# Reading the first half of an output projection out of PSUM: one VectorE addition, or a ScalarE copy and a POOL addition

## The chip, the cores and the metric

The kernel runs on one NeuronCore of a Trainium2 chip. The metric is the time of one execution on the device in microseconds (us), the median over several runs. The core's engines are TensorE (PE: matmuls and transposes, which write to PSUM), VectorE (DVE), ScalarE (ACT), GpSimd (POOL) and the DMA queues, most of them issued by SyncE (SP). Each engine works through its own queue of instructions in order and waits for the others by semaphores. PSUM holds the results of PE in eight banks; SBUF holds everything else.

## The reference, cut to what matters

Two layers of a decoder trunk on x of 512 tokens by 1024 features in float32. Each layer has one input projection, three groups of heads beside each other, one output projection that is added to x, and a SwiGLU feed-forward block that is added to x.

```python
for l in range(DEPTH):                                   # DEPTH = 2
    h = rmsnorm(x, attn_norm[l])
    (q, kc, vc, ksl, ...) = split_columns(h @ w_in[l])
    o_nsa = nsa_mixer(...)                               # 512 features: attention
    o_gla = gla_mixer(...)                               # 256 features: linear attention
    o_sg = spatial_gating(...)                           # 256 features
    x = x + jnp.concatenate([o_nsa, o_gla, o_sg], axis=-1) @ w_out[l]
    h = rmsnorm(x, ffn_norm[l])
    x = x + (jax.nn.silu(h @ w_gate[l]) * (h @ w_up[l])) @ w_down[l]
return rmsnorm(x, final_norm)
```

The rows of `w_out` that belong to o_gla and o_sg (the second 512 of 1024) need nothing of o_nsa. That half of the product can be computed while attention still runs.

## The kernel before, in words

x is kept transposed in SBUF for the whole kernel, in the tile `xT`: 8 blocks of 128 features by 512 tokens, float32. Matrix products are made with split operands: a weight block of 128 x 1024 is loaded into a tile `raw` by SP (L327), ACT copies it to the rounded part `hl[:, 0]` (L318), DVE subtracts to get the rest `hl[:, 1]` (L321). `mm3` (L336 to L338) then makes three matmuls of 128 x 512 for each block of 128 features.

The mixer of a layer ends with attention over eight heads (L1188 to L1290). For each head and each of two branches PE makes the scores (L1215, L1216, L1234, L1235), DVE finds the row maxima (L1218, L1237), ACT takes the exponentials and their sums (L1222, L1239), DVE makes the scale factors (L1244, L1245), and the four blocks of P are scaled: two by DVE (L1253), one by ACT (L1251), the largest by POOL (L1249). POOL's scaling is ordered behind DVE's by a dependency written out by hand (L1255). PE then transposes the blocks (L1262), ACT and DVE read the transposes out as a split pair `PT` (L299, L300), and PE multiplies with V (L1275, L1276). At a head's end ACT and DVE add up its output (L1288, L1289), and each pair of heads is split into one half of a tile of `okt` (L1290 by way of L299 and L300). POOL also copies queries for later heads (L1186).

The output projection `out_proj` is called twice for each layer, after the mixer in the program's text (L1673, L1675): first with `k0 = 4`, `kts = None`, `nrm = None` for the contraction rows 4 to 7, which come from the other two head groups and are ready when attention begins, then with `k0 = 0` for rows 0 to 3, which are attention's own. Each call goes through eight blocks of output features; a block takes four `mm3` into one bank of PSUM, and `residual_out` reads the bank out:

```python
def residual_out(m, ps, gcols, kts, nrm, late=False):
    nc.vector.tensor_tensor(xT[:, m, :], xT[:, m, :], ps, op=ALU.add)   # L500
    if nrm is not None:
        ...
```

The first call uses ring "g" of PSUM, two banks that take turns, so a third block can start only when the first has been read out. The second call's first two blocks use the same ring.

The order of work is not that of the text. The framework lays out each engine's queue when the program is built: it goes by priorities (the text's order, raised where `tc.high_priority` stands), by its own estimates of durations, and by when operands and buffers are free. So the first call of `out_proj`, late in the text, fills holes within attention: its matmuls run where PE would stand idle, and its L500 where DVE has a gap in that estimate. Dependencies are added from what instructions read and write, and each engine's order is fixed from then on.

Two small buffers of 128 x 512 float32 in SBUF matter for the change. Tag "nsq" holds squares for the sums of the next norm (L351 to L353: ACT squares, POOL adds to `nacc`). Tag "rb" holds a norm's factor spread over the partitions (L370, L371). There is one buffer of each. During attention neither is in use: "rb" was last read by the projections before it, "nsq" by the norm of the layer before.

Of the kernel before, what the change touches and what calls it, by code (L numbers as in the profile page):

```python
# [10 lines left out]
F32 = mybir.dt.float32  # L11
# [5 lines left out]
ALU = mybir.AluOpType  # L17
AX = mybir.AxisListType

P = 128  # L20
SEQ = 512
# [122 lines left out]
def trunk_kernel(ctx: ExitStack, tc: tile.TileContext, a, out):  # L144
    nc = tc.nc
# [5 lines left out]
    sm = ctx.enter_context(tc.tile_pool(name="sm", bufs=1))  # L151
# [3 lines left out]
    def nm(s):  # L155
        uid[0] += 1
        return f"{s}_{uid[0]}"
# [7 lines left out]
    def psum(tag):  # L165
        taken[tag] += 1
        return banks[:, rings[tag][(taken[tag] - 1) % len(rings[tag])], :]
# [78 lines left out]
    def g_ffn(l):  # L246
        return vec[:, 16 + 8 * l : 24 + 8 * l]
# [9 lines left out]
    xT = cp.tile([P, KT, SEQ], F32, name="xT")  # L257
# [35 lines left out]
    def split_scaled(kt, kk, src, gcol):  # L293
        last_hi[:] = [nc.scalar.activation(kt[:, kk, 0, :], src, AF.Copy, scale=gcol)]
        nc.vector.scalar_tensor_tensor(kt[:, kk, 1, :], src, gcol, kt[:, kk, 0, :].bitcast(F32),  # L295
                                       op0=ALU.mult, op1=ALU.subtract)
# [8 lines left out]
    def site(name):  # L305
        wsite[:] = [name, 0]
# [17 lines left out]
    def w_rows(mat, r0, nk, c0, w, pri=WPRI, raw=None, hl=None):  # L324

        def loads(raw):
            nc.sync.dma_start(raw[:, 0 : nk * w].rearrange("p (k c) -> p k c", k=nk),  # L327
                              mat[r0 : r0 + nk * P, c0 : c0 + w].rearrange("(k p) c -> p k c", p=P))
        hl = w_unit(nk * w, loads, pri, raw, hl)
        return hl[:, :, 0 : nk * w].rearrange("p s (k c) -> p s k c", k=nk)  # L330
# [4 lines left out]
    def mm3(ps, lh, ll, rh, rl, start, stop, skip=False):  # L335
        nc.tensor.matmul(ps, lh, rh, start=start, stop=False, skip_group_check=skip)  # L336
        nc.tensor.matmul(ps, lh, rl, start=False, stop=False, skip_group_check=skip)  # L337
        return nc.tensor.matmul(ps, ll, rh, start=False, stop=stop, skip_group_check=skip)  # L338
# [159 lines left out]
# [5 lines that stand above are left out]
            if kts is not None:  # L503
                split_scaled(kts[m // 2], m % 2, xT[:, m, :], gcols[:, m : m + 1])
            if not late:
                nrm.add(xT[:, m, :])
# [786 lines left out]
    def out_proj(l, okt, k0, kts, nrm, tags=None):  # L1293
        tags = tags or ATAGS

        site("o%d" % k0)
        for mq in range(KT // 2):
            u = w_rows(a["w_out"][l], k0 * P, 4, mq * 256, 256)
            for b in range(2):
                ps = psum(tags[2 * mq + b])  # L1300
                for kk in range(4):
                    o_ = okt[(k0 + kk) // 2]
                    mm3(ps, u[:, 0, kk, b * P : (b + 1) * P], u[:, 1, kk, b * P : (b + 1) * P],
                        o_[:, kk % 2, 0, :], o_[:, kk % 2, 1, :], kk == 0, kk == 3)
                residual_out(2 * mq + b, ps, g_ffn(l), kts, nrm, mq > 1)
        if nrm is not None:

            with tc.issue_after(last_hi[0].ins):
                for m in range(4, KT):
                    nrm.add(xT[:, m, :])  # L1310
# [358 lines left out]
    for l in range(L):  # L1669
        okt = mixer(l, norm, xkt, eu if l == 0 else None)  # L1670
        fnorm = Norm()
        with tc.tile_pool(name=f"ff{l}", bufs=1, reuse_waits="tile") as fp:
            out_proj(l, okt, 4, None, None)  # L1673
            fkt = [kt_tile() for _ in range(4)]
            out_proj(l, okt, 0, fkt, fnorm, BTAGS)  # L1675
            ops = Ops(g_ffn(l), fkt, fp)
            if l < L - 1:
                norm = Norm()
                xkt = []
                ffn(l, fp, fnorm, fkt, ops, xkt, norm, g_attn(l + 1))  # L1680
            else:
                ffn(l, fp, fnorm, fkt, ops, None, None, None)
# [24 lines left out]
```

## Time and profile before

| what | value |
|---|---|
| time, median of 3 runs | 1287.74 us (1286.69 to 1287.77) |
| the profiled execution: time | 1286.52 us |
| the profiled execution: span from first to last instruction | 1284.7 us |
| mean granted TensorE clock | 0.997 of full speed |
| L500, whole kernel | 56 additions, 37.5 us on DVE |
| of these by the first call of `out_proj` | 8 a layer, between 173.3 and 238.2 us and between 803.7 and 868.6 us |
| attention, layer 0 and layer 1 | about 167.5 to 283.0 us and 797.9 to 913.4 us |

Rows of the profile are read so. A group's row has the line, the engine, the operation, output<-inputs by the program's names, the shapes, the count, then busy us and mean ns of one, then the idle time of the engine just before these instructions and what ended it. A timeline row has start, duration, engine, line and operation; in brackets stands the idle time before it and what ended that. A row of a table of stretches has its length, and for each engine the busy us and the number of instructions, then the granted clock, the share of DMA time and GB/s. A row of waits has who waited for what, the total us, the number of times and the longest.

### The profile page before, as it was taken

To read this page: it belongs to the slowest core of one execution; us is meant where nothing else is said; L and a number is where in the kernel's file an instruction comes from. 1 tells how busy PE (TensorE), PEld (TensorE's weight loads), DVE (VectorE), ACT (ScalarE), POOL (GpSimd) and SP (SyncE) were. 2 spreads that over 40 slices of the span, in tenths; PEclk is the share of its full clock that TensorE was granted. 3 is DMA by queue.
4 is the path that set the end of the run, shared out by engine and by line. 5 is a ranking of instruction groups with operands and counts; after the bars stand their busy time and mean duration, and the time that the engine had idled before them with its cause. 6 is when DMAs were issued, how large, how long until landed. Compare 5 with 4: busy or idle time off the path is not lost. (4 is left out here: it accounts for less than half of the span.)

```text
span 1284.7 us, 18046 instructions
## 1 busy us (share of the span) xinstructions
PE 1257.3 (98%) x6678; PEld 1038.5 (81%) x6678; DVE 918.2 (71%) x1645; ACT 677.0 (53%) x1288; POOL 160.5 (12%) x157
## 2 busy tenths in 40 slices
PE   8999999999999999999999999999999999999997
PEld 7888788778888888888888877777788888888886
DVE  6767799977856775587446678998767457827775
ACT  6675367864533553354346733788544445515532
POOL 0101222122000100010301012121210001000102
PEclk9999999999999999999999999999999999999999
DMA  6451441034335885483434317210533448754811
GB/s 231 142 180 34 115 108 33 17 87 127 98 105 141 197 232 146 111 200 99 115 94 149 116 34 175 64 33 3 146 98 99 131 117 210 216 130 133 227 66 66
DMA packets 134204, 155.01 MB, mean 121 GB/s; under 512 B 9307, under 2 KB 86885, under 8 KB 134117
## 3 DMA queue, kind: packets, MB, share of 16 engines
q1 hardware_dynamic: 117392, 128.81, 33.3%
q0 software_dynamic: 10208, 20.84, 9.2%
q10 hardware_dynamic: 6516, 4.22, 1.5%
q8 instruction: 52, 0.85, 0.3%
q14 instruction: 36, 0.29, 0.1%
HBM read 149.92 MB, written 2.10 MB: 118 GB/s over the span
## 5 line engine op out<-in xcount | busy, mean ns | idle before, releaser
L318 ACT CAST hl<-raw 128x1024 fp32r<-128x1024 f32 (+3 forms) x170 | 175.2, 1035 | 226.5 <-PE banks L338 160.9
L321 DVE TENSOR_TENSOR hl<-raw,hl 128x1024 fp32r<-128x1024 f32 (+3 forms) x170 | 207.1, 1222 | 94.6 <-ACT hl L318 93.0
L336 PE MATMUL banks<-hl,kt 128*128 128x512 f32 (+2 forms) x688 | 257.9, 375 | 1.1 <-ACT hl L318 1.1
L337 PE MATMUL banks<-hl,kt 128*128 128x512 f32 (+2 forms) x688 | 256.4, 373 | 0.0
L338 PE MATMUL banks<-hl,kt 128*128 128x512 f32 (+2 forms) x688 | 256.1, 373 | 0.0
L337 PE MATMUL banks<-kt,hl 128*128 128x512 f32 x384 | 151.5, 394 | 0.0
L338 PE MATMUL banks<-kt,hl 128*128 128x512 f32 x384 | 151.1, 394 | 0.0
L336 PE MATMUL banks<-kt,hl 128*128 128x512 f32 x384 | 150.4, 394 | 0.0
L336 PEld LDWEIGHTS banks<-hl,kt 128*128 128x128 f32 x688 | 129.5, 188 | 23.6 <-ACT hl L318 1.9
L337 PEld LDWEIGHTS banks<-hl,kt 128*128 128x128 f32 x688 | 129.5, 188 | 21.8 <-DVE hl L321 0.3
L338 PEld LDWEIGHTS banks<-hl,kt 128*128 128x128 f32 x688 | 129.4, 188 | 21.7
L318 ACT CAST hl<-wx 128x1024 fp32r<-128x1024 f32 x48 | 50.5, 1052 | 79.8 <-PE banks L338 69.1
L337 PEld LDWEIGHTS banks<-kt,hl 128*128 128x128 f32 x384 | 72.2, 188 | 14.7 <-DVE kt L295 0.9
L338 PEld LDWEIGHTS banks<-kt,hl 128*128 128x128 f32 x384 | 72.3, 188 | 13.7
L336 PEld LDWEIGHTS banks<-kt,hl 128*128 128x128 f32 x384 | 72.0, 188 | 13.3 <-ACT kt L299 0.3
L321 DVE TENSOR_TENSOR hl<-wx,hl 128x1024 fp32r<-128x1024 f32 x48 | 58.7, 1224 | 18.4 <-ACT hl L318 18.2
L500 DVE TENSOR_TENSOR xT<-xT,banks 128x512 f32<-128x512 f32 x56 | 37.5, 681 | 47.6 <-PE banks L338 47.6
L337 PE MATMUL banks<-act,hl 128*128 128x512 f32 x172 | 67.0, 390 | 0.0
L338 PE MATMUL banks<-act,hl 128*128 128x512 f32 x172 | 66.9, 389 | 0.0
L336 PE MATMUL banks<-act,hl 128*128 128x512 f32 x172 | 66.9, 390 | 0.0
L300 DVE TENSOR_TENSOR PT<-banks,PT 128x384 fp32r<-128x384 f32 (+1 forms) x96 | 54.6, 597 | 14.1 <-ACT PT L299 13.2
L336 PE MATMUL banks<-hl,act 128*128 128x512 f32 (+1 forms) x164 | 63.0, 384 | 0.0
(356 smaller groups left out, 2404.1 us busy)
## 6 DMA issues: line engine op xcount, KB each, us to landing
raw<-in_w_gate_dram SPq DMA_DIRECT2D x44, 512.0 KB, 3.9
raw<-in_w_up_dram SPq DMA_DIRECT2D x44, 512.0 KB, 4.0
raw<-in_w_in_dram SPq DMA_DIRECT2D x32, 512.0 KB, 3.7
raw<-in_w_down_dram SPq DMA_DIRECT2D x36, 256.0 KB, 4.0
raw<-in_w_down_dram SPq DMA_DIRECT2D x18, 512.0 KB, 3.7
raw<-in_w_out_dram SPq DMA_DIRECT2D x16, 512.0 KB, 4.3
raw<-in_cmp_w_k_dram SPq DMA_DIRECT2D x8, 512.0 KB, 3.9
raw<-in_cmp_w_v_dram SPq DMA_DIRECT2D x8, 512.0 KB, 4.9
```

The lines of the kernel that those rows point to most:

```text
L300: nc.vector.tensor_tensor(lo, src, hi.bitcast(F32), op=ALU.subtract)
L318: last_cast[:] = [nc.scalar.copy(hl[:, 0, 0:n], raw[:, 0:n])]
L321: e_.tensor_tensor(hl[:, 1, 0:n], raw[:, 0:n], hl[:, 0, 0:n].bitcast(F32), op=ALU.subtract)
L336: nc.tensor.matmul(ps, lh, rh, start=start, stop=False, skip_group_check=skip)
L337: nc.tensor.matmul(ps, lh, rl, start=False, stop=False, skip_group_check=skip)
L338: return nc.tensor.matmul(ps, ll, rh, start=False, stop=stop, skip_group_check=skip)
L500: nc.vector.tensor_tensor(xT[:, m, :], xT[:, m, :], ps, op=ALU.add)
```

## The change

In the first call of `out_proj` (the one with `nrm is None`) the DVE addition L500 is replaced by two instructions: ACT copies the PSUM bank to a tile `part` in SBUF, and POOL adds `part` to the block of `xT` in place. The tiles `part` take turns between the buffers of tags "nsq" and "rb". The second call, and all other calls of `residual_out`, are as before.

```diff
-                residual_out(2 * mq + b, ps, g_ffn(l), kts, nrm, mq > 1)
+                if nrm is None:
+                    part = sm.tile([P, SEQ], F32, tag=("nsq", "rb")[b], name=nm("part"), bufs=1)
+                    nc.scalar.copy(part, ps)
+                    nc.gpsimd.tensor_tensor(xT[:, 2 * mq + b, :], xT[:, 2 * mq + b, :], part, op=ALU.add)
+                else:
+                    residual_out(2 * mq + b, ps, g_ffn(l), kts, nrm, mq > 1)
```

## The prediction

> **What bounds the kernel now.** I read the engines' shares first, then a table of the time by stages, then inside attention the instruction groups of VectorE (DVE) and its waits, and last the timeline around the lines of the change.
>
> ```profile
> PE 1257.3 (98%) x6678; PEld 1038.5 (81%) x6678; DVE 918.2 (71%) x1645; ACT 677.0 (53%) x1288; POOL 160.5 (12%) x157
> ```
>
> TensorE (PE) is busy for 98% of the span, so the kernel as a whole is bound by it. So the question is where PE could be fed better by the other engines.
>
> ```profile
> core 0: us, PE busy (x) PEld busy (x) DVE busy (x) ACT busy (x) POOL busy (x), PEclk, DMA share, GB/s
> 167.50:238.50 71.00, 68.53 (x387) 55.61 (x386) 66.89 (x147) 54.46 (x145) 13.27 (x16) 1.00 0.21 60
> 797.90:868.90 71.00, 68.53 (x387) 55.65 (x386) 66.88 (x147) 54.47 (x145) 13.27 (x16) 1.00 0.20 60
> 238.50:283.00 44.50, 41.63 (x227) 31.81 (x226) 33.92 (x76) 31.61 (x85) 9.72 (x9) 1.00 0.25 60
> 868.90:913.40 44.50, 41.63 (x227) 31.81 (x226) 33.92 (x76) 31.61 (x85) 9.71 (x9) 1.00 0.26 60
> ...
> 283.00:797.90 514.90, 512.25 (x2685) 426.28 (x2684) 347.87 (x563) 245.04 (x395) 58.48 (x52) 1.00 0.50 131
> ```
>
> The first four rows are attention, in two stretches for each of the two layers; the last row is most of the rest. Outside attention PE is busy for 512 of 515 us: nothing is to be won there by moving work of other engines. In attention's first 71 us, where the half of the output projection that the change touches runs as filler, DVE is busy for 66.9 us (94%), ScalarE (ACT) for 54.5 (77%), POOL for 13.3 (19%). In the next 44.5 us no engine but PE is above 77%. The layers agree to 0.02 us, so they run one order of instructions 630.4 us apart, and whatever the change does to one it does to both.
>
> That DVE sets the pace of the first stretch is seen in its waits there, and in what stands before L500:
>
> ```profile
> DVE PT L300 <- ACT PT L299: 1.5, 2, 0.8
> DVE qst L1126 <- ACT qst L1125: 0.7, 2, 0.6
> DVE nmx L1218 <- PE banks L1216: 0.2, 1, 0.2
> DVE nmx L1237 <- PE banks L1235: 0.2, 1, 0.2
> DVE tmp L1289 <- ACT tmp L1288: 0.2, 1, 0.2
> ...
> L500 DVE TENSOR_TENSOR xT<-xT,banks 128x512 f32<-128x512 f32 x8 | 5.4, 674 | 0.0
> ```
>
> The columns of the waits are total us, times, longest. They sum to 2.8 us of 71: DVE hardly ever waits. The group row is that of the eight L500 additions of one layer: 5.4 us busy, 674 ns each, and 0.0 us of idle time before them, so each stands in a backlog and holds up what is behind it. The backlog also holds PSUM:
>
> ```profile
> 226.67 0.40 PE L337 MATMUL banks<-kt,hl 128*128 128x512 f32 x1
> 226.90 0.39 PE L338 MATMUL banks<-kt,hl 128*128 128x512 f32 x1
> ...
> 236.85 0.68 DVE L500 TENSOR_TENSOR xT<-xT,banks 128x512 f32<-128x512 f32 x1
> ...
> 237.53 0.66 DVE L500 TENSOR_TENSOR xT<-xT,banks 128x512 f32<-128x512 f32 x1
> ...
> 239.09 0.40 PE L336 MATMUL banks<-kt,hl 128*128 128x512 f32 x1
> ```
>
> The filler's last matmul starts at 226.9, its two banks of ring "g" are read out only at 236.85 and 237.53, and the next filler, the other half of the projection, starts on them at 239.1. For some 12 us PE has no filler.
>
> **The change part by part.** *Removed:* 16 additions on DVE (eight a layer), 16 x 0.674 = 10.8 us, 5.4 a layer, all in the stretch where DVE is the bound.
>
> *Added on ACT:* 16 copies of a PSUM bank to SBUF. The same form stands in the trace:
>
> ```profile
> L1566 ACT COPY zb<-banks 128x512 f32<-128x512 f32 x12 | 7.0, 590 | 8.3 <-PE banks L338 8.3
> L1109 POOL TENSOR_TENSOR qr<-qr,tmp 128x512 f32<-128x512 f32 x6 | 9.8, 1635 | 13.7 <-DVE nt L275 6.6 <-DVE tmp L1106 6.4 <-DVE oss L1053 0.7
> 159.94 1.28 POOL L1109 TENSOR_TENSOR qr<-qr,tmp 128x512 f32<-128x512 f32 x1 [3.31 <-DVE nt L275]
> 165.44 2.34 POOL L1109 TENSOR_TENSOR qr<-qr,tmp 128x512 f32<-128x512 f32 x1 [3.19 <-DVE tmp L1106]
> ```
>
> 8 x 0.59 = 4.7 us a layer come into the 71 - 54.5 = 16.5 us that ACT is idle. They fit, but an instruction that arrives while a copy runs is late by up to 0.59, on average half: at most 8 x 0.3 = 2.4 us a layer, at least nothing. DVE's largest wait above is for ACT's L299, so part of this comes back to DVE. I take 1.0 us a layer, nearer the low end, since a third of ACT's idle time is enough to hold the copies.
>
> *Added on POOL:* 16 additions of two SBUF operands. The L1109 rows (a group, then two of its six from the timeline) are an addition of the same shape: 1.28 us when undisturbed, 2.34 when not. 8 x 1.28 = 10.2 us bring POOL to 23.5 of 71 us. The length costs nothing by itself: nobody reads x of these rows until the other half adds to it after 284 us. The bank is free after the copy, and the copy after next, which reuses the same `part` buffer, comes two groups later, 24 matmuls on. What queues behind an addition that waits for its copy are POOL's own casts of q (L1186) and scalings of P (L1249), and for L1249 wait the transposes L1262 on PE.
>
> *Added between POOL and DVE:* L500 read one operand from PSUM, the POOL addition reads both from SBUF. In the trace POOL and DVE hold each other up when both read two SBUF operands:
>
> ```profile
> 191.85 1.04 POOL L1249 TENSOR_TENSOR P<-P,rr 128x512 f32<-128x512 f32 x1 [7.53 <-DVE P L1253]
> 192.22 1.75 DVE L321 TENSOR_TENSOR hl<-raw,hl 128x1024 fp32r<-128x1024 f32 x1
> 231.54 1.22 DVE L321 TENSOR_TENSOR hl<-raw,hl 128x1024 fp32r<-128x1024 f32 x1
> ...
> L321 DVE TENSOR_TENSOR hl<-raw,hl 128x1024 fp32r<-128x1024 f32 x7 | 9.1, 1296 | 0.2
> L1245 DVE TENSOR_TENSOR rr<-rr,gates 128x4 f32<-128x4 f32 x16 | 4.3, 268 | 0.1
> 234.32 0.16 DVE L1245 TENSOR_TENSOR rr<-rr,gates 128x4 f32<-128x4 f32 x1
> ...
> L1249 POOL TENSOR_TENSOR P<-P,rr 128x512 f32<-128x512 f32 x16 | 16.6, 1040 | 62.4 <-DVE P L1253 25.5 <-ACT P L1239 14.8 <-ACT P L1251 7.8
> L295 DVE SCALAR_TENSOR_TENSOR kt<-xT,vec,kt x16: 739/742/1791, 288.4 to 932.1; 128x512 fp32r<-128x512 f32 x16
> ```
>
> L321 took 1.75 us beside a POOL scaling that was still running, 1.22 alone. In one layer's attention the sixteen L1249 cost DVE 7 x (1.296 - 1.22) on L321 and 16 x (0.268 - 0.16) on L1245, 0.5 + 1.7 = 2.3 us, or 0.14 us each. The worst single case is L295: 1.79 against 0.74, 1.05 us for one POOL addition. So one new addition costs DVE 0.14 to 1.05 us; I take 0.3, nearer the first, since that was measured in the same stretch, and above it, since the kernel orders L1249 by hand behind a DVE scaling while the new addition may fall anywhere. That is 2.4 us a layer.
>
> The Trainium skill, "SBUF — State Buffer", section "Who interferes with whom", says why: GpSimd's only SBUF ports are DVE's second pair, held as a lock, and a DVE instruction with two SBUF inputs contends with a GpSimd instruction that reads SBUF. The trace agrees (1.75 against 1.22 us). By that page L500, with one SBUF input, never contended, so the contention is wholly new.
>
> No DMA and no queue of SP is touched. No matmul is added.
>
> *The sum,* per layer: 5.4 off DVE, less 2.4 for the shared reads, less 1.0 for ACT: 2.0 us. PE allows it: it is booked for 68.5 of the 71 us, so even by its bookings 2.5 us a layer are free, and bookings overlap: the matmul at 226.67 above is booked for 0.40 us and the next starts 0.23 us after it. Two layers: 4.0 us. The profiled execution's 1286.52 us (span 1284.7, 1.8 around it) would become 1282.5; it lies 1.2 below the median of the three runs, and the same 4.0 off 1287.74 gives **1283.7 us**. By the low ends (0.14, nothing on ACT) it is 5.4 - 1.1 = 4.3 a layer, 1279.1; with no loss at all 1276.9. By the high ends (1.05, 2.4) it is 5.4 - 8.4 - 2.4 = -5.4 a layer, 1298.5.
>
> **The rivals.** A difference within 0.2% (2.6 us) can't be told from none by a measurement of this kernel.
>
> *Nothing comes of it.* The loss on the shared reads eats the relief: at 0.55 us an addition, between my value and the worst row, 8 x 0.55 + 1.0 = 5.4, and the time stays at 1287.7. For it speaks that seven L321 of 1.22 us and many small operations of two SBUF inputs lie in the stretch; against it the 0.14 us of L1249. The Trainium skill, "Perfetto Trace Analysis", section "Optimizing Scalar/DVE Operations", warns of this: where DVE is saturated it may make sense to give work to Scalar or GPSIMD, but GPSIMD and DVE share a read port, so moving work between these two might not help. On this case's rows that rule is half right: DVE is saturated (94%), and the price is 0.14 us in the nearest rows, not a whole instruction.
>
> *Slower: the new instructions get in front of the chain.* The planner lays the queues anew, and POOL or ACT runs in order. An addition ahead of an L1249 holds it up by up to 1.28 us, and the four transposes of that group, PE's in-order queue and the next ACT copy with it. PE waits for L1249 already:
>
> ```profile
> PE banks L1262 <- POOL P L1249: 1.2, 4, 0.5
> ACT P L1251 <- DVE rr L1245: 2.9, 3, 1.5
> ```
>
> The first row: four waits in a layer's attention, 1.2 us in all, 0.5 the longest. If four of the eight additions fall so, 4 x 1.28 = 5.1 us a layer replace the gain of 2.0: 3.1 a layer worse, 1293.9 with both layers. It decides from two such places a layer, where the gain is gone (2.6 against 2.0); with three the kernel is measurably slower (7.7 - 4.0 = 3.7 us, 1291.4). For it: ten of the sixteen L1249 are in the same 71 us. Against: POOL is idle for 81% of it. One more ACT wait of the length of the second row, 1.5 us, at two places a layer does about the same (1289.7).
>
> *All of it comes through.* The additions find DVE at other work, the copies fit ACT's gaps, and the banks of the last two groups come free up to 9 us sooner, so that the other half's matmuls fill PE's holes there: 10.8 us, 1276.9. Against it: ACT is busier than 77% just where the last groups end.
>
> That the work is not moved at all can't be: both calls name their engine.
>
> **How the numbers follow.** Faster by 2.6 to 10.8 us, the forecast and its better end: 0.46. Within 2.6 us: 0.26. Slower: 0.28, 0.18 for POOL or ACT in front of the chain and 0.10 for shared reads dearer than 0.67 us an addition (5.4/8), where DVE itself loses. The range of 8 in 10 goes from 1277.0, the case without loss, to 1293.0, just short of four delayed scalings a layer; 0.08 lies below and 0.12 above.
>
> **What would show it.** L500 should stand at 40 additions instead of 56, sixteen ACT copies near 0.59 us and sixteen POOL additions of 1.28 us or somewhat more at the new lines. Right: DVE's busy time in the 71 us falls by 3 to 4 us, the last attention step (L1289, the split L300 behind it) comes about 2 us sooner in each layer, and the distance of the layers shrinks from 630.4 to about 628. L321 above 1.5 us beside new additions shows the shared reads. Wrong: PE's or L1262's waits for POOL above 3 us a layer, DVE's waits for ACT well above 2.8 us in the stretch, or an order of the attention steps that is no longer the old one, with single waits of over 2 us: then the planner's new order, not the moved microseconds, made the time.

## The result, and the profile after

The changed kernel takes 1297.18 us (median of 4 runs, 1296.93 to 1297.53), the kernel before 1287.76 in the 4 runs beside them: a ratio of 1.0074 [1.0056, 1.0091], 9.4 us slower. 1283.7 was predicted, and 1293.0 was the upper end of the range. The profiled execution took 1297.21 us (span 1295.4, against 1284.7).

The engines' shares of the changed kernel, and the groups of the instructions that the change touches:

```profile
PE 1259.9 (97%) x6678; PEld 1039.2 (80%) x6678; DVE 917.5 (71%) x1629; ACT 686.2 (53%) x1304; POOL 185.9 (14%) x173
```

```profile
L1307 ACT COPY part<-banks 128x512 f32<-128x512 f32 x16 | 9.6, 602 | 3.1 <-PE banks L338 3.1
L1308 POOL TENSOR_TENSOR xT<-xT,part 128x512 f32<-128x512 f32 x16 | 23.2, 1452 | 32.0 <-ACT part L1307 32.0
```

The change does what it says: 16 copies of 0.60 us on ACT, 16 additions of 1.45 us on POOL, 16 instructions fewer on DVE. But DVE is busy for 917.5 us where it was 918.2. Sixteen additions of 0.674 us went away, 10.8 us; only 0.7 of it is missing from its busy time. Other DVE instructions last longer: L1245 takes 12.7 us in all instead of 8.6, L1253 23.3 instead of 20.0.

To find the place I cut both spans at the same events: the last norm step before attention (L1057), the ends of the first, third, fourth and eighth head (L1289), and the first scale factors of the feed-forward block (L1412, in the changed kernel L1417). Columns as in the prediction's table of stretches. The kernel before:

```profile
162.55:200.20 37.65, 36.96 (x204) 30.49 (x203) 35.59 (x71) 25.96 (x63) 6.67 (x6) 1.00 0.36 96
200.20:224.60 24.40, 23.94 (x144) 19.95 (x143) 22.59 (x47) 19.79 (x52) 5.54 (x7) 1.00 0.08 22
224.60:238.40 13.80, 12.47 (x69) 9.29 (x68) 13.53 (x37) 11.71 (x35) 3.13 (x4) 1.00 0.14 40
238.40:281.20 42.80, 39.93 (x220) 30.51 (x219) 32.92 (x74) 31.04 (x85) 9.72 (x9) 1.00 0.24 55
281.20:316.05 34.85, 34.82 (x157) 28.04 (x156) 24.65 (x39) 17.33 (x25) 9.38 (x7) 1.00 0.39 113
...
316.05:792.95 476.90, 474.28 (x2511) 395.43 (x2512) 319.40 (x520) 225.26 (x368) 47.03 (x44) 1.00 0.50 133
```

The changed kernel:

```profile
164.46:203.40 38.94, 36.18 (x197) 29.15 (x195) 33.90 (x63) 27.06 (x63) 12.82 (x10) 1.00 0.33 92
203.40:228.60 25.20, 24.51 (x146) 20.22 (x146) 23.36 (x48) 21.73 (x57) 8.98 (x10) 1.00 0.08 22
228.60:244.60 16.00, 14.51 (x81) 11.08 (x80) 14.36 (x37) 13.75 (x38) 6.80 (x7) 1.00 0.12 35
244.60:286.70 42.10, 38.03 (x211) 29.11 (x211) 32.41 (x73) 30.56 (x83) 9.13 (x9) 1.00 0.25 57
286.70:321.50 34.80, 34.80 (x157) 27.98 (x156) 24.66 (x40) 17.32 (x24) 9.35 (x7) 1.00 0.39 113
...
321.50:799.86 478.36, 475.71 (x2511) 396.35 (x2512) 319.62 (x520) 225.33 (x368) 47.07 (x44) 1.00 0.50 133
```

The first five rows are layer 0's attention with what follows it: 157.04 us against 153.50, **3.54 us longer**, and all of it is lost up to the fourth head (1.29 + 0.80 + 2.20), where the new instructions run; afterwards 0.75 come back. In layer 1 the same stretch takes 157.36 against 153.47, 3.89 longer. Together that is 7.4 of the 10.7 us between the two spans. The rest lies where no instruction differs: 1.9 us ahead of L1057 in layer 0 (164.46 against 162.55) and 1.5 between the two attentions (478.36 against 476.90), of which the last section tells.

### The profile page after: what moved, and what is told of

It is laid out like the page before. It is cut to its first block, busy times and chain, and to the rows that moved or that the text cites. A ratio compares the mean times of both kernels' runs of the same rounds, so it can differ in the third digit from the quotient of the medians.

```text
span 1295.4 us, 18078 instructions
## 1 busy us (share of the span) xinstructions
PE 1259.9 (97%) x6678; PEld 1039.2 (80%) x6678; DVE 917.5 (71%) x1629; ACT 686.2 (53%) x1304; POOL 185.9 (14%) x173
## 4 chain that ended last, share of the span: by engine, by line
PE 68%; DVE 5%; ACT 4%; issue 1%; DMA 1%; POOL 0%; ACTq 0%; DVEq 0%
PE banks L336 20%; PE banks L337 20%; PE banks L338 20%; PE banks L1262 1%; PE banks L1275 1%; PE banks L1604 1%; PE banks L1276 1%; DMA raw<-in_w_in_dram 1%; ACT hl L318 1%; DVE PT L300 1%; ACT P L1239 0%; DVE hl L321 0%; DVE rr L1245 0%; DVE P L1253 0%; DVE nmx L1237 0%
## 5 line engine op out<-in xcount | busy, mean ns | idle before, releaser
L321 DVE TENSOR_TENSOR hl<-raw,hl 128x1024 fp32r<-128x1024 f32 (+3 forms) x170 | 206.1, 1217 | 87.6 <-ACT hl L318 85.6
L321 DVE TENSOR_TENSOR hl<-wx,hl 128x1024 fp32r<-128x1024 f32 x48 | 58.7, 1224 | 22.4 <-ACT hl L318 22.2
L337 PE MATMUL banks<-hl,act 128*128 128x512 f32 (+1 forms) x164 | 63.0, 384 | 0.0
L336 PE MATMUL banks<-hl,act 128*128 128x512 f32 (+1 forms) x164 | 63.0, 384 | 0.0
```

What stands on the lines that cost most here:

```text
L321: e_.tensor_tensor(hl[:, 1, 0:n], raw[:, 0:n], hl[:, 0, 0:n].bitcast(F32), op=ALU.subtract)
```

## The experiments

"Layer" in the table is the stretch from L1057 to the feed-forward block's first scale factors in the profiled execution, less that of the kernel before (153.50 and 153.47).

| kernel | time, us | beside it, before | ratio | layer 0 | layer 1 |
|---|---|---|---|---|---|
| the change | 1297.18 | 1287.76 | 1.0074 [1.0056, 1.0091] | +3.54 | +3.89 |
| copy_only | 1289.06 | 1287.24 | 1.0013 [1.0003, 1.0022] | +0.60 | +2.16 |
| copy_dve | 1287.65 | 1287.24 | 1.0006 [0.9995, 1.0016] | +0.14 | +0.15 |
| pool_memset | 1289.72 | 1287.24 | 1.0020 [1.0011, 1.0030] | +0.91 | +0.87 |
| pinned | 1290.24 | 1287.24 | 1.0027 [1.0017, 1.0037] | +1.69 | +1.67 |
| no_read | 1287.33 | 1287.41 | 0.9997 [0.9988, 1.0007] | -0.30 | -0.27 |
| dve_twice | 1296.24 | 1287.41 | 1.0067 [1.0050, 1.0085] | +3.49 | +3.54 |
| pool_extra | 1291.29 | 1287.41 | 1.0034 [1.0022, 1.0046] | +2.09 | +2.03 |
| halves | 1295.12 | 1287.41 | 1.0062 [1.0045, 1.0079] | +3.07 | +3.09 |
| thin | 1297.58 | 1287.68 | 1.0074 [1.0059, 1.0089] | +2.24 | +5.61 |
| thin_no_read | 1293.41 | 1287.68 | 1.0035 [1.0020, 1.0050] | +3.14 | +2.33 |

Layer 1 of copy_only, both layers of thin_no_read and layer 1 of thin were disturbed: PE's granted clock was halved there for some microseconds. In copy_only this fell at 814.1 us, and the stretch to the first head, 37.05 us at full clock in layer 0, took 38.48:

```profile
793.52:832.00 38.48, 37.43 (x197) 30.76 (x195) 32.02 (x62) 26.97 (x63) 6.77 (x6) 0.96 0.34 91
```

So copy_only is read from its layer 0 below.

One thing makes some of these comparisons sharp. The planner lays every queue anew, so a kernel and its variant mostly differ in more than the edit. But the traces show that in these stretches **the change, copy_only, halves and pool_memset run one and the same order on PE, DVE and ACT**, instruction by instruction, and differ on POOL alone; so do the kernel before and pool_extra. POOL's own older instructions keep their order as well. What differs between the kernels of one such family is what stands between them on POOL and nothing else. The two families' orders differ from each other in some forty places on PE.

**copy_only** keeps ACT's copy and leaves POOL's addition out.

```diff
-                    nc.gpsimd.tensor_tensor(xT[:, 2 * mq + b, :], xT[:, 2 * mq + b, :], part, op=ALU.add)
```

> The ScalarE copy stays, the POOL addition is left out (so x lacks the first half of the projection). If the loss of 9.4 us is made by the shared SBUF reads of POOL and DVE (theory A) or by POOL's queue, additions standing in front of the scalings L1249 (theory B), it goes with the additions, and the relief of DVE remains: 1280 to 1285 us. If it is made by the copies on ScalarE or by the new order of the queues that the planner lays out once L500 is gone (theory C), the time stays near that of the change: 1294 to 1298 us.

1289.06 us, between the two ranges that I had expected. Without the POOL additions 7.6 of the 9.4 us of slowdown are gone, although DVE has the same work as in the changed kernel; the relief that the lower range counted on doesn't show. Its stretches in layer 0:

```profile
162.75:199.80 37.05, 36.01 (x197) 29.26 (x195) 32.04 (x63) 26.91 (x63) 6.82 (x6) 1.00 0.35 96
199.80:225.00 25.20, 24.37 (x146) 20.25 (x146) 22.83 (x48) 21.75 (x57) 6.53 (x8) 1.00 0.08 23
225.00:240.00 15.00, 14.33 (x81) 11.15 (x80) 13.28 (x37) 13.38 (x38) 3.73 (x5) 1.00 0.13 37
240.00:282.10 42.10, 38.06 (x212) 29.14 (x211) 32.37 (x72) 30.53 (x84) 9.17 (x9) 1.00 0.24 57
```

Against the changed kernel, in the same order of PE, DVE and ACT, the eight additions cost 1.89 us up to the first head, nothing to the third, 1.00 to the fourth, nothing to the eighth: 2.94 in all (157.04 less the 154.10 of copy_only). The trace of the changed kernel has the instructions. The timeline rows of four of POOL's eight additions, of what DVE runs beside each, and of the scaling L1249 behind the first:

```profile
183.42 1.56 DVE L1253 TENSOR_SCALAR P<-P,rr 128x128 f32<-128x128 f32 x2
183.53 1.31 POOL L1308 TENSOR_TENSOR xT<-xT,part 128x512 f32<-128x512 f32 x1 [4.31 <-ACT part L1307]
185.06 1.04 POOL L1249 TENSOR_TENSOR P<-P,rr 128x512 f32<-128x512 f32 x1 [0.23 <-DVE P L1253]
...
198.30 1.22 DVE L321 TENSOR_TENSOR hl<-raw,hl 128x1024 fp32r<-128x1024 f32 x1
198.52 2.16 POOL L1308 TENSOR_TENSOR xT<-xT,part 128x512 f32<-128x512 f32 x1 [3.19 <-ACT part L1307]
199.64 1.06 DVE L1245 TENSOR_TENSOR rr<-rr,gates 128x4 f32<-128x4 f32 x1
...
207.24 1.29 POOL L1308 TENSOR_TENSOR xT<-xT,part 128x512 f32<-128x512 f32 x1 [0.37 <-ACT part L1307]
207.63 1.24 DVE L1253 TENSOR_SCALAR P<-P,rr 128x128 f32<-128x128 f32 x2
...
229.99 1.29 POOL L1308 TENSOR_TENSOR xT<-xT,part 128x512 f32<-128x512 f32 x1 [1.30 <-ACT part L1307]
230.14 1.15 DVE L1245 TENSOR_TENSOR rr<-rr,gates 128x4 f32<-128x4 f32 x1
```

and the rows of three of these instructions in copy_only:

```profile
182.39 1.04 POOL L1249 TENSOR_TENSOR P<-P,rr 128x512 f32<-128x512 f32 x1 [4.90 <-DVE P L1253]
...
196.95 0.17 DVE L1245 TENSOR_TENSOR rr<-rr,gates 128x4 f32<-128x4 f32 x1
...
204.05 0.54 DVE L1253 TENSOR_SCALAR P<-P,rr 128x128 f32<-128x128 f32 x2
```

A multiplication of 128 x 4 numbers takes 1.06 us instead of 0.17, another one 1.15, a pair of scalings 1.24 instead of 0.54, and the first pair 1.56. Where a single instruction is hit, it ends with POOL's addition (200.70 and 200.68, 231.29 and 231.28); the first pair ends 0.14 us after it (184.98 and 184.84), the other pair 0.34. DVE stands still until POOL is done. The Trainium skill, "SBUF — State Buffer", section "Who interferes with whom", says that the shared pair of ports is an exclusive lock and that the order of issue decides who blocks. These rows agree. With 0.55 us for an undisturbed pair the first two places lose 1.0 and 0.9 us, which is the 1.89 of the first stretch; the fourth loses 1.0, the 1.00 of the third. The third place's 0.7 us is hidden. L321, for which the prediction looked out, isn't longer (1.22): it had come first, and the addition beside it took 2.16.

At the first place a second cause can't be told apart from the held-up DVE: the addition also stands ahead of the scaling L1249 on POOL. Counted from L1057, L1249 starts at 19.64 us in copy_only and at 20.60 in the changed kernel, and the addition ends at 20.38. POOL's queue by itself would thus have made 0.74 of these 0.96 us. At the second and fourth place POOL is idle for 1.8 and 1.6 us before the next L1249, so there it is DVE alone.

**copy_dve** keeps ACT's copy and adds on DVE, now from SBUF.

```diff
-                    nc.gpsimd.tensor_tensor(xT[:, 2 * mq + b, :], xT[:, 2 * mq + b, :], part, op=ALU.add)
+                    nc.vector.tensor_tensor(xT[:, 2 * mq + b, :], xT[:, 2 * mq + b, :], part, op=ALU.add)
```

> The copy on ScalarE, the addition from SBUF on DVE instead of POOL: DVE has its 0.69 us for each addition again, POOL has none. Theory A and theory B: no more than the price of the copies against the kernel before, 1287 to 1291 us. Theory C: the loss stays, 1294 us or more.

1287.65 us, no measurable difference from the kernel before. DVE has its sixteen additions again, and the time isn't above that of copy_only, where they are left out: the first sign that DVE's microseconds weren't what counted, though in another order of the queues.

**pool_memset** puts two fills of `part` in the place of the addition. POOL is busy, and reads nothing.

```diff
-                    nc.gpsimd.tensor_tensor(xT[:, 2 * mq + b, :], xT[:, 2 * mq + b, :], part, op=ALU.add)
+                    for _ in range(2):
+                        nc.gpsimd.memset(part, 0.0)
```

> In place of each POOL addition POOL fills the tile part twice (2 x 0.56 us, which writes SBUF and reads nothing; x lacks the first half of the projection). POOL is occupied about as long as by the addition. Theory A: DVE's instructions with two SBUF inputs (L1245, L321) no longer wait, 1282 to 1288 us. Theory B: the scalings L1249 stand behind the fills as they did behind the additions, 1294 to 1298 us. Theory C: 1294 us or more too, but then copy_only and copy_dve are slow as well.

1289.72 us, above the range of 1282 to 1288 that counted on the relief. In the order of copy_only the fills cost 0.31 us a layer, the additions 2.94. DVE's groups inside the attention of one layer, first copy_only, then pool_memset, then the changed kernel:

```profile
L1253 DVE TENSOR_SCALAR P<-P,rr 128x256 f32<-128x256 f32 x16 | 5.5, 346 | 0.0
L1245 DVE TENSOR_TENSOR rr<-rr,gates 128x4 f32<-128x4 f32 x16 | 4.4, 273 | 0.3
```

```profile
L1253 DVE TENSOR_SCALAR P<-P,rr 128x256 f32<-128x256 f32 x16 | 6.2, 385 | 0.0
L1245 DVE TENSOR_TENSOR rr<-rr,gates 128x4 f32<-128x4 f32 x16 | 4.3, 269 | 0.3
```

```profile
L1253 DVE TENSOR_SCALAR P<-P,rr 128x256 f32<-128x256 f32 x16 | 6.6, 410 | 0.0
L1245 DVE TENSOR_TENSOR rr<-rr,gates 128x4 f32<-128x4 f32 x16 | 6.3, 396 | 0.3
```

L1245, with two SBUF inputs, is not touched by fills that only write (269 against 273 ns), but is by additions that read (396). L1253 is touched by both. So at the second and fourth place, where L1245 is held up and 1.9 of the 2.94 us arise, it is not POOL's occupation that costs the time, it is what POOL reads. For the first place the fills are no such test: a single fill of 0.52 us stands ahead of L1249 there, where the addition took 1.31.

**pinned** is the change with each addition ordered on POOL behind one of POOL's scalings L1249, which itself stands behind a scaling of DVE.

```diff
+PIN = (0, 0, 1, 3, 4, 5, 7, 8)
...
+                            p3s.append(p3)
...
-                    nc.gpsimd.tensor_tensor(xT[:, 2 * mq + b, :], xT[:, 2 * mq + b, :], part, op=ALU.add)
+                    add = nc.gpsimd.tensor_tensor(xT[:, 2 * mq + b, :], xT[:, 2 * mq + b, :], part, op=ALU.add)
+                    tc.add_manual_dep(add.ins, p3s[PIN[2 * mq + b]].ins.name,
+                                      mybir.DependencyInfo(mybir.DependencyClass.NoSync, mybir.DependencyReason.DATA), reason="behind a scaling")
```

> The change with each POOL addition ordered behind one of the scalings L1249 (the 1st, 1st, 2nd, 4th, 5th, 6th, 8th and 9th of a layer), so that it starts when DVE has just done its own scalings L1253 and the next L1249 is microseconds away. Theory A and theory B: most of the loss goes, 1284 to 1290 us, and no L1253 or L1245 of DVE is above 0.7 us beside an addition. Theory C: the planner lays out another order again, and the time can be anywhere from 1286 to 1298 us, whatever the additions meet.

1290.24 us, just above the range of 1284 to 1290: the same work on the same engines, 6.9 us less than the change. The DVE scalings and POOL's additions in the attention of one layer (in this file L1249 is the L1245 of before, L1257 its L1253):

```profile
L1257 DVE TENSOR_SCALAR P<-P,rr 128x256 f32<-128x256 f32 x16 | 5.5, 346 | 0.0
L1249 DVE TENSOR_TENSOR rr<-rr,gates 128x4 f32<-128x4 f32 x16 | 4.8, 300 | 0.2
L1313 POOL TENSOR_TENSOR xT<-xT,part 128x512 f32<-128x512 f32 x16 | 20.4, 1284 | 0.0
```

The scalings are back at 346 ns, L1245 at 300, and an addition takes 1.28 us instead of 1.45. This points to the places into which the additions fall as most of their price. It doesn't prove it: the order of PE and DVE differs from that of the change here, so the 6.9 us are not the additions' alone.

**no_read** is the kernel before, with the first half not read out at all.

```diff
-                residual_out(2 * mq + b, ps, g_ffn(l), kts, nrm, mq > 1)
+                if nrm is not None:
+                    residual_out(2 * mq + b, ps, g_ffn(l), kts, nrm, mq > 1)
```

> The first half's results are not read out at all: no copy, no addition (x lacks the first half of the projection), so DVE loses 10.8 us of work and ScalarE and POOL get none. If the 16 additions L500 stood in holes of DVE's queue, in which DVE would otherwise have waited for TensorE's scores (theory H), nothing is won: 1286 to 1289 us. If they held DVE up and the copies on ScalarE ate what their removal won (theory R), it shows here: 1279 to 1284 us.

1287.33 us, 0.9997 [0.9988, 1.0007]. All 10.8 us are off DVE, nothing is added anywhere, and nothing is gained: 0.3 us a layer. In the order that the planner lays out for it, the prediction's first term is not there. Its stretches:

```profile
162.56:199.30 36.74, 36.13 (x201) 29.89 (x199) 33.06 (x66) 26.07 (x63) 6.68 (x6) 1.00 0.36 97
199.30:223.40 24.10, 23.53 (x142) 19.47 (x141) 22.10 (x45) 20.05 (x51) 5.48 (x7) 1.00 0.08 23
223.40:238.90 15.50, 14.98 (x83) 11.83 (x82) 13.39 (x38) 12.67 (x37) 3.79 (x5) 1.00 0.12 36
238.90:281.00 42.10, 38.03 (x211) 29.13 (x210) 32.41 (x73) 30.53 (x83) 9.10 (x9) 1.00 0.25 57
```

Up to the third head 1.2 us are indeed won (0.9 + 0.3). Between the third and the fourth PE then does 83 matmuls instead of 69, and the fourth head ends 1.7 us later after the third than before; the last four heads have 9 matmuls less and win 0.7. The planner laid filler there. It is likely, but not shown, that the filler held up the chain (scores, maxima, exponentials, scalings and transposes of the next head): thin, below, takes 15.42 us for this stretch with 67 matmuls. And DVE waits more: 5.3 us in the prediction's 71, where it was 2.8. The two longest entries:

```profile
DVE nmx L1237 <- PE banks L1235: 1.4, 4, 0.6
DVE qst L1126 <- ACT qst L1125: 1.2, 1, 1.2
```

**dve_twice** is the kernel before with a second, unused addition of the same kind ahead of each of the eight L500 of a layer.

```diff
+                if nrm is None:
+                    part = sm.tile([P, SEQ], F32, tag=("nsq", "rb")[b], name=nm("part"), bufs=1)
+                    nc.vector.tensor_tensor(part, xT[:, 2 * mq + b, :], ps, op=ALU.add)
                 residual_out(2 * mq + b, ps, g_ffn(l), kts, nrm, mq > 1)
```

> The kernel before with a second addition of the same form for each L500, into the tile part, on DVE: 10.8 us more of DVE's work in the same places. Theory H: what is left of the holes takes up more than half of it, 1288 to 1292 us. If DVE's queue had no holes there (what the prediction assumed), all of it comes out at the end: 1296 to 1299 us.

1296.24 us. This lies in the range for a DVE queue without holes, and by its time alone it looks like an engine that is the bound: 5.4 us more on DVE, 3.5 a layer slower. The stretches (to the fourth head, to the eighth, to the feed-forward block) say otherwise:

```profile
164.19:239.40 75.21, 70.07 (x389) 55.46 (x388) 71.63 (x153) 57.09 (x146) 15.36 (x16) 1.00 0.20 55
239.40:282.20 42.80, 40.17 (x224) 31.48 (x223) 36.83 (x81) 31.90 (x85) 7.29 (x7) 1.00 0.11 38
282.20:321.18 38.98, 38.98 (x177) 31.87 (x176) 23.20 (x40) 17.87 (x24) 12.49 (x9) 1.00 0.52 135
```

No head is late: the fourth comes 0.64 us sooner than before (75.21 against 75.85), the four others take the same 42.80. The planner put the additions off instead: the last L500 of the first call starts at 277.4 us, where it was 237.5. What is longer is the time after the last head, 38.98 against 34.85, with 177 matmuls instead of 157. The banks of ring "g" were read out later, and some 20 matmuls of it were left for the time after attention, when PE has nothing to wait for.

**pool_extra** is the kernel before, L500 in its place, with one POOL addition of two SBUF operands (the same block twice) behind each; its result isn't used.

```diff
                 residual_out(2 * mq + b, ps, g_ffn(l), kts, nrm, mq > 1)
+                if nrm is None:
+                    part = sm.tile([P, SEQ], F32, tag=("nsq", "rb")[b], name=nm("part"), bufs=1)
+                    nc.gpsimd.tensor_tensor(part, xT[:, 2 * mq + b, :], xT[:, 2 * mq + b, :], op=ALU.add)
```

> The kernel before with L500 on DVE as it was, and behind each L500 one POOL addition of the same size as the change's, both operands the block of xT, into the tile part, which nobody reads. Nothing else is changed, and ScalarE gets no copies. Theory A (an addition holds up DVE through the shared reads, about 0.45 us each): 1291 to 1296 us, with L1253 or L1245 of about 1 us beside additions. If the additions cost nothing by themselves and the loss of the change lay in the copies and the new order together: 1286 to 1289 us.

1291.29 us. In the unchanged order of PE, DVE and ACT, eight POOL additions cost 2.09 us a layer, 0.26 each. Not all of it is the shared read. At the first head the scaling L1249 starts right behind an addition on POOL, 1.14 us later after L1057 than before, while DVE's scalings L1253 are only 0.43 us late. There POOL's queue, the prediction's rival, is most of the loss. At another place L321 takes 2.09 us beside an addition instead of 1.23, as the prediction had looked out for.

**halves** is the change with each addition cut into two of 256 columns.

```diff
-                    nc.gpsimd.tensor_tensor(xT[:, 2 * mq + b, :], xT[:, 2 * mq + b, :], part, op=ALU.add)
+                    for c in (slice(0, 256), slice(256, 512)):
+                        nc.gpsimd.tensor_tensor(xT[:, 2 * mq + b, c], xT[:, 2 * mq + b, c], part[:, c], op=ALU.add)
```

> The change with each POOL addition made as two of 256 columns. POOL's work stays the same or grows, but one instruction holds DVE for about 0.7 us instead of 1.29. Theory A: each hit costs about half, 1291 to 1295 us. If the cost is POOL's time in front of the scalings L1249 (theory B), it stays: 1296 to 1299 us.

1295.12 us. Same order again: the additions cost 2.47 us a layer (3.07 - 0.60) instead of 2.94. That is at the upper end of what I expected if the hold-ups were halved. One hold-up is shorter, but there are twice as many (821 ns each, in place of 1452). And at the first place both halves stand ahead of L1249 on POOL: it starts 0.88 us late against copy_only, though DVE's second scaling there ends only 0.47 late.

```profile
L1245 DVE TENSOR_TENSOR rr<-rr,gates 128x4 f32<-128x4 f32 x16 | 5.2, 325 | 0.3
...
L1309 POOL TENSOR_TENSOR xT<-xT,part 128x256 f32<-128x256 f32 x32 | 25.6, 821 | 32.0 <-ACT part L1307 32.0
```

**thin** and **thin_no_read** ask whether PE's own load is the bound. In the kernel before each `mm3` of the first half does one matmul instead of three (64 fewer a layer); thin_no_read leaves the reading out besides, as no_read does.

```diff
-                    mm3(ps, u[:, 0, kk, b * P : (b + 1) * P], u[:, 1, kk, b * P : (b + 1) * P],
-                        o_[:, kk % 2, 0, :], o_[:, kk % 2, 1, :], kk == 0, kk == 3)
+                    if nrm is None:
+                        nc.tensor.matmul(ps, u[:, 0, kk, b * P : (b + 1) * P], o_[:, kk % 2, 0, :], start=kk == 0, stop=kk == 3)
+                    else:
+                        mm3(...)
```

> The kernel before with one matmul instead of three in each mm3 of the first half (the two correction products are left out): 64 matmuls less a layer, 64 x 0.227 = 14.5 us of TensorE's work within attention, and everything else as it was, L500 on DVE too. This is the basis for thin_no_read. If TensorE's own queue bounds attention's first stretch as much as DVE does (theory P, which would explain why the removal of L500 won nothing), a part of the 29 us is won, 1265 to 1284 us; if DVE alone bounds it, nothing: 1286 to 1288 us.

> thin without the 16 additions L500 and without anything in their place. Theory P: with TensorE relieved, DVE is the bound, and the removal now shows: 5 to 10 us below thin. If L500 stands in holes that come from the chain of dependencies (scores, maxima, exponentials, transposes) whatever TensorE does (theory H in its narrow form): less than 2 us below thin.

1297.58 us: with 128 matmuls less the kernel is 9.9 us slower, outside both ranges. Layer 0 of thin, at full clock:

```profile
164.03:319.77 155.74, 138.90 (x722) 106.34 (x721) 129.38 (x265) 107.09 (x255) 34.85 (x32) 1.00 0.27 71
```

PE is booked for 138.90 us instead of 148.12, and the stretch takes 155.74 instead of 153.50. So in this order PE's load is not what fills the time; for the order of before this isn't shown. The planner's order of thin differs from that of before in over fifty places on PE, and why it is worse was not found; the halved clock in layer 1 is a part of it. thin_no_read, 1293.41 us, 4.2 below thin and so between its two ranges, ran at 1288.0 to 1296.4 us. In its profile, as in thin's layer 1, PE's clock was halved for some microseconds within attention (a mean of 0.93 in the stretch below), so the two don't tell what L500 is worth when PE has less to do.

```profile
160.00:238.50 78.50, 68.75 (x347) 53.18 (x346) 69.20 (x142) 54.64 (x137) 16.66 (x18) 0.93 0.29 70
```

## Why the prediction was wrong

**The relief, 5.4 us a layer, is the step that failed.** It stood on the sentence "0.0 us of idle time before them, so each stands in a backlog and holds up what is behind it", and on DVE being busy for 94% of the stretch. Idle time of zero says that DVE had an instruction to do just before. It doesn't say that the one behind was ready and late for it. Taken out altogether (no_read), L500 brings 0.3 us a layer, and DVE's waits grow from 2.8 to 5.3 us; doubled (dve_twice), it delays no head, it is put off. That fits instructions of the last priority which the planner lays where DVE would have waited. The reason stays partly open, though: each of these kernels has an order of its own, and no pair here differs in DVE's work alone. That PE sets the time instead (booked for 69.3 of the 71 us in no_read) isn't ruled out; thin speaks against it, in an order of its own too. The rival "all of it comes through" expected the banks to come free sooner and PE's holes to be filled; in no_read filler did come sooner, and nothing was won.

**The shared reads, 2.4 us a layer, were sized nearly right**: 2.94, in an order held fixed, 0.37 an addition against the 0.30 that I took, within my bounds of 0.14 and 1.05. Up to 0.74 of it may be POOL's queue. But I took it as a small loss for every addition, spread over L321 and L1245. It is 0.7 to 1.0 us in four of eight places, on short instructions of the chain, and the number comes near mine only because the other four hit nothing. That is luck.

**ACT, 1.0 us a layer:** copy_only less no_read is 0.60 + 0.30 = 0.9. The size agrees, but these two run different orders. In copy_dve, with the same copies and DVE's additions, a layer is only 0.15 us longer than before. So the price of the copies is not pinned down.

**The sum.** By the measured terms a layer is -0.3 + 0.9 + 2.94 = 3.5 us longer, as its profile has it (+3.54). They add up by the way they were taken, as differences of the same profiles. I had -2.0. Of the 5.5 us between them 5.1 are the relief.

**The rivals.** The rival of POOL in front of the chain has a part in it. PE's waits for POOL's scalings in one layer's attention of the changed kernel:

```profile
PE banks L1262 <- POOL P L1249: 2.0, 5, 0.7
```

That is 2.0 us against 1.2, below the 3 us that I had set as its mark. But it wasn't for nothing: it can be 0.74 us of the 2.94 here, at the first place, and it is most of the first loss in pool_extra and halves. The rival of dear shared reads names the right mechanism but not the point from which it decides: I had put that at 0.67 us an addition, which is 5.4/8; with a relief of 0.3 and 0.9 for ACT, any price makes the kernel slower. Two slips don't bear on the outcome: nine, not ten, of the sixteen L1249 lie in the 71 us, and the three chances add up to 1 and leave nothing for the 0.08 below 1277.0.

**The marks.** Right: both layers act nearly alike (+3.54 and +3.89), and the counts and durations of the new instructions. The new order of the planner's, which I had named as a sign of being wrong, is there too. Wrong: DVE's busy time hardly falls, L1289 comes later, and L1057 of the two layers is 635.4 us apart instead of 630.4, where I had expected 628. Of the Trainium skill's rule on saturated engines ("Perfetto Trace Analysis", "Optimizing Scalar/DVE Operations") I had written that DVE is saturated; no_read shows that its 94% were not a bound that could be relieved.

**What stays open.** In the profiles 7.4 us are lost in the two attentions, and the medians differ by 9.4. The other 2.0 aren't explained; the profiles show differences outside these stretches, where the change has no instruction, and the next but one section has them. And a difference of half a microsecond a layer (copy_only against copy_dve) is within what a new order of the planner's does by itself.

## What to carry to other kernels

Before work is moved off an engine that looks full, take the work out altogether and time that: a busy share of 94% and an idle time of zero don't tell by themselves that the engine is the bound. A POOL instruction that reads SBUF can hold up DVE's smallest two-input instruction for nearly its whole length (1.15 us beside an addition of 1.29), and the POOL work queued behind it too, so count which DVE instructions of the chain will stand beside it, not its average price; where it must be on POOL, try putting it by hand behind a POOL instruction that DVE has just fed (pinned, 1290.2 against 1297.2 us, in an order of its own). None of the versions tried is faster than the kernel before.

## What the runs showed of the hardware beside that

In most of the profiles PE's granted clock is halved somewhere ahead of the last stretch, for 3.4 us or twice that. In the kernel before it falls into the loading at the start, in the changed one into the mixer of layer 1:

```profile
8.00:11.40 3.40, 3.40 (x11) 2.79 (x11) 2.79 (x4) 2.76 (x6) 0.00 (x0) 0.51 1.03 377
```

```profile
707.00:710.40 3.40, 3.40 (x9) 2.23 (x8) 0.17 (x1) 2.21 (x3) 1.15 (x2) 0.51 0.76 240
```

The second accounts for most of the 1.5 us between the two attentions. It lies at 703 to 707 us in copy_dve, dve_twice, halves and thin_no_read too, and in these five that stretch takes 477.8 to 478.4 us; in the others it takes 476.5 to 476.9, but for thin with 477.8. In copy_only a second halving falls into layer 1's attention; pinned, pool_extra and pool_memset have none before the last 10 us. The start of L1057 in layer 0 moves between 162.6 and 164.5 us in the profiles, and it is earliest in those three that have the halving at the start (before, copy_only, no_read). Why, and whether the change takes part in it, wasn't tried.
